# Two more blocks of a gated-linear-attention head turned by transposing transfers instead of by TensorE

## The chip, the cores and the metric

The kernel runs on one core of one Trainium2 chip. The metric is device time in microseconds (us) for one execution, the median of several runs; less is better. TensorE (PE) multiplies matrices into PSUM, VectorE (DVE) and ScalarE (ACT) do the elementwise work, GpSimd (POOL) computes a few square roots here, and SyncE (SP) issues most transfers. ACT issues some transfers too. Each engine runs its own list of instructions in a fixed order, so an instruction that has to wait holds up everything behind it on that engine.

## The reference

A decoder trunk of two layers over 16 learned meta tokens and 512 input tokens, width 1024: first a gated linear attention (GLA) layer with 4 heads, then a differential softmax attention layer with 8 heads, then a final RMSNorm. The part that matters here is the end of the GLA layer. For every head, `o` (528 tokens by 512 columns) is normed by row, multiplied with a gate made from `z`, and multiplied with the output weights:

```python
    o = head_rms(o.transpose(0, 2, 1, 3)).reshape(B, L, D_INNER) * gnorm.astype(f32)
    y = jax.nn.silu(z.astype(f32)) * o
    return (y.astype(xn.dtype) @ w_out)
```

All inputs and outputs are fp32.

## The kernel before, in words

**Layout.** Activations are held transposed: features on the 128 partitions, tokens along the free dimension (`hT`, `s.z`, `s.y`). A product needs its fp32 operands split into a high and a low part, both in the fp32r type; `split` (L261 to 273) does this with one ACT copy (the high part, L270) and one DVE subtraction (the low part, L271), and the product is the sum of three matmul passes.

**Blocks.** The tokens of a head are worked in five blocks (`BLK`): block 0 is the 16 meta tokens, blocks 1 to 4 are 128 tokens each; the last four are the large ones. `gla_blocks` (L1215) goes over them in order. `output(b)` (L1222) multiplies scores and values into a PSUM tile (`ps`; L391, L1233), takes the mean square on ACT (L1236), the inverse root on DVE and POOL (L532, L533), and writes the scaled rows `on` to SBUF (ACT, L1238). The rows stand with tokens on the partitions and have to be turned for the output product.

**Two ways to turn a block.** `rows(b, on)` (L1285) does it on TensorE: four transposes of 128x128 into a PSUM tile (L1291), a DVE product with the gate `s.z` straight from PSUM (L1293), and a split. `far_rows` (L1242) does it for a pair of blocks by transfer: for each block, `leave` copies `on` on ACT so that the two 16-bit halves of each word are apart (L1252, out<-in `t<-t`) and sends them to DRAM from the ACT queue (L1253, `yd<-t`); then `turn` issues one transposing transfer on the SP queue for the pair (L1259, `keep<-yd`), which lands in a part of the buffer `keep` (`b_all`); then `scaled_rows`, once for each block, multiplies in place with the gate on DVE (L1266) and splits. Before the change, blocks 1 to 4 of the second head (`hd == 1`) go by transfer and everything else by `rows`.

**What sets the order.** The program is written out by a generator, the weaver `W`. Attention steps are written where they stand in the code; between them `W.fill(us)` takes pieces of weight products from a queue worth that many estimated microseconds. `W.follow` puts a step behind a stretch of such work: `turn` comes 4.0 us of woven work after the second block has left, and `scaled_rows` a written number of microseconds after that. PE runs exactly in written order. The order on DVE and ACT is set by a scheduler from the written order and priorities; steps marked `urgent` go earlier. `far_rows` is not marked, its `leave` is.

**What runs beside it.** The weight products are `Unit`s (L419 to 511), a seven-product scheme on quarter blocks. Each Unit has partial sums in PSUM tiles `bx`, `by`, `bv`. PE adds p7 to `bx`; ACT copies this partial sum out (`u`, L443); DVE combines it with `bv` (L468); and only after that may PE go on adding p3 into the same `bv` (L422). This is a chain PE, ACT, DVE, PE, and other work of PE (the first product of the next Unit and p4) stands between. Weights come as `raw` tiles (two buffers; SP, L292 and L279), are summed (`sum`, L357) and split to `wh`/`wl` and `a11`, `a12`, `a22`. During the first head's blocks the queue holds the second head's query and key Units; then `q_gla_v(1)` follows, two Units for the second head's values (`t`), then the first head's output product (`q_gla_out(0)`, L959), with the second head's `gla_scores` (L1158: `kd` at L1162 and L1163, score products at L1170 and L1178) and the small `second_layer_setup` (L1076, L1077, L1082) woven in.

Of the kernel before, what the change touches and what calls it, by code (L numbers as in the profile page):

```python
# [209 lines left out]
def trunk(ctx, tc, x, meta, g_norm, gla_w_in, gla_w_gate_up, gla_b_gate, gla_gnorm, gla_w_out,  # L210
# [21 lines left out]
    def T(p, shape, dt, tag, **kw):  # L232
        uid[0] += 1
        return p.tile(shape, dt, tag=tag, name=f"{tag}_{uid[0]}", **kw)
# [68 lines left out]
    W = Weaver()  # L303
# [252 lines left out]
    def tmp():  # L556
        return T(tp, [P, L], F32, "t")


    def words(t):  # L560

        return t.bitcast(U16)
# [203 lines left out]
    for k0 in range(0, KT, 2):  # L766
        if k0 + 2 < KT:
            scaled_pair(k0 + 2)
        i, ks = k0 // 4, slice(k0 % 4, k0 % 4 + 2)
# [210 lines left out]
    for k in range(KT):  # L980
        for n in range(2):
            for i, x in enumerate((X["b11"], b12) if k < 4 else (X["b21"], X["b22"])):
                if k == 0:
                    warm_up((3, 3, 1, 4)[2 * n + i], idle)
                if (k, 2 * n + i) in turns_of:
                    b, half = turns_of[k, 2 * n + i]
# [228 lines left out]
    def gla_blocks(hd, s, fill, last, far):  # L1215
# [25 lines left out]
        def far_rows(pair):  # L1241

            yd = T(dp, [2, P, 2, 512], U16, "yd", bufs=2)
            src = yd.rearrange("m p h c -> (m p h) c")
            i = pair[0] - 1
            raw = b_all[:, i:i + 2, :].rearrange("p m c -> p (m c)")[:, :8 * P].rearrange("p (m c) -> p m c", m=4)
            left = [0, 1]

            @urgent
            def leave(j, on):  # L1250
                pl = words(tmp()[:, :512]).rearrange("p (h c) -> p h c", h=2)
                act.activation(pl, words(on).rearrange("p (c h) -> p h c", h=2), AF.Copy)  # L1252
                act.dma_start(yd[j], pl)  # L1253
                left.remove(j)
                if not left:
                    W.follow((4.0, turn), tag=s)

            def turn():
                tc.keep_in_program_order(sp.dma_start(words(raw), src, transpose=True))  # L1259
                W.follow((10.5 if i == 0 else 16.5, lambda: scaled_rows(0)), (1.5, lambda: scaled_rows(1)), tag=s)  # L1260

            def scaled_rows(j):
                t0, n = BLK[pair[j]]
                y = raw[:, :, j * P:(j + 1) * P]
                with tc.issue_after(W.mark.ins):
                    dve.tensor_tensor(y, y, s.z[:, :, t0:t0 + n], op=ALU.mult)  # L1266
                    for m0, m1, hi, lo in s.groups:
                        split(hi[:, :, t0:t0 + n], lo[:, :, t0:t0 + n], y[:, m0:m1, :])

            return leave  # L1270
# [27 lines left out]
        prev, leave = None, None  # L1298
        for b in range(5):
            W.fill(0.6 if b == 0 else 1.9 if b == 1 else fill[0])  # L1300
            if prev is not None and (b == 1 or not far):
                rows(b - 1, prev)
            prev = output(b)
            if far and b:
                if b % 2:
                    leave = far_rows((b, b + 1))
                leave(1 - b % 2, prev)
            W.fill(fill[1] if b else 1.6)
        if not far:
            W.fill(2.0)  # L1310
            rows(4, prev)

# [17 lines left out]
    for hd in range(G_HEADS):  # L1330
        s = heads[hd]
        last = hd == G_HEADS - 1
# [28 lines left out]
        else:  # L1361
            W.stop = q_gla_v(hd + 1, heads[hd + 1])
        W.land()
        far = hd == 1
        gla_blocks(hd, s, (1.2, 1.2) if last else (0.6, 1.2) if far else (1.9, 1.6), last, far)
        W.finish()
        W.stop = None

# [441 lines left out]
    s = heads[0]  # L1810
# [14 lines left out]
    for hd in range(D_HEADS):  # L1825
        last = hd == D_HEADS - 1
        s = heads[hd]
# [114 lines left out]
```

## Time and profile before

| | |
|---|---|
| median of three runs | 982.9 us (982.31 to 983.34) |
| profiled execution | 981.49 us, of which its span 979.7 us |
| granted TensorE clock, mean | 0.998 |
| PE busy | 965.9 us (99%) |
| DVE busy | 777.5 us (79%) |
| ACT busy | 621.3 us (63%) |
| four transposes of one large block on PE (L1291) | 0.60 us from first start to last end |
| DVE product with the gate (L1293 from PSUM, L1266 from SBUF) | 0.68 us each |
| ACT copy into halves (L1252) | 1.06 us |

The span is the time from the first to the last instruction. Times in a timeline are counted from the span's start; a row gives start, duration, engine, line, operation, out<-in, shapes and a count, and in square brackets how long the engine was idle before it and who ended that. Rows of matmuls overlap: the next group starts before the modelled end of the last, so that the cost of a group on PE is read from start to start. DVE and ACT rows overlap a little too, and are read in the same way. The first head's blocks are worked from about 106 to 138 us, the second head's from about 210 to 236 us.

### The profile page before, as it was taken

The numbers are of one execution on the slowest core, as the hardware profiler recorded it, in microseconds if no ns is written. First come the engines' busy times: TensorE is split into PE (matmuls) and PEld (weight loads), VectorE is DVE, ScalarE is ACT, GpSimd is POOL, SyncE is SP. The second block draws the span as 40 slices with busy tenths as digits, with TensorE's granted clock in tenths as the row PEclk, the third lists the DMA queues.
The fourth block names the chain that finished last, engine by engine and source line by source line (L and its number), as shares of the span: only waits on it lengthen the run. The fifth ranks groups of instructions, "written<-read, shape, count | busy, mean of one in ns | idle before, by whom it ended". The sixth has DMA issues, their size and how long they took to land. (4 is left out here: it accounts for less than half of the span.)

```text
span 979.7 us, 18153 instructions
## 1 busy us (share of the span) xinstructions
PE 965.9 (99%) x7049; PEld 913.1 (93%) x7049; DVE 777.5 (79%) x1584; ACT 621.3 (63%) x1310; POOL 50.3 (5%) x68
## 2 busy tenths in 40 slices
PE   9999999999999999999999999999999999999997
PEld 8999999999999999998999998898998999988896
DVE  7889885887888797566997985977958879677785
ACT  7775755577647656546757774575764667655573
POOL 1000000000000100000001001001010000000001
PEclk9999999999999999999999999999999999999999
DMA  7322224625363122212323425135252351622212
GB/s 195 87 85 61 77 71 130 153 91 129 121 153 120 52 87 87 82 49 87 98 87 106 129 78 156 48 97 140 80 147 86 98 136 53 181 65 77 87 65 86
DMA packets 113226, 98.37 MB, mean 100 GB/s; under 512 B 37341, under 2 KB 99069, under 8 KB 113136
## 3 DMA queue, kind: packets, MB, share of 16 engines
q1 hardware_dynamic: 109680, 90.66, 31.9%
q10 hardware_dynamic: 3456, 6.51, 1.9%
q8 instruction: 57, 0.93, 0.4%
q14 instruction: 33, 0.27, 0.1%
HBM read 83.64 MB, written 8.62 MB: 94 GB/s over the span
## 5 line engine op out<-in xcount | busy, mean ns | idle before, releaser
L271 DVE TENSOR_TENSOR wl<-raw,wh 128x1024 fp32r<-128x1024 f32 x98 | 119.6, 1222 | 24.7 <-ACT wh L270 16.3
L270 ACT ACTIVATE wh<-raw 128x1024 fp32r<-128x1024 f32 x98 | 103.1, 1054 | 52.1 <-PE by L959 23.7
L422 PE MATMUL bv<-x,wh 128*128 128x264 f32 (+1 forms) x656 | 97.8, 287 | 0.8 <-DVE z L470 0.6
L422 PE MATMUL bx<-x,wh 128*128 128x264 f32 (+1 forms) x640 | 95.3, 287 | 0.6 <-ACT u L443 0.4
L422 PEld LDWEIGHTS bv<-x,wh 128*128 128x128 f32 x656 | 86.4, 189 | 1.5 <-DVE z L470 0.9
L422 PEld LDWEIGHTS bx<-x,wh 128*128 128x128 f32 x640 | 84.5, 189 | 2.3 <-ACT u L443 1.2
L443 ACT ACTIVATE u<-bx 128x264 f32<-128x264 f32 (+1 forms) x120 | 45.4, 379 | 28.6 <-PE bx L422 24.9
L271 DVE TENSOR_TENSOR wl<-sum,wh 128x1024 fp32r<-128x1024 f32 x41 | 50.1, 1222 | 15.7 <-ACT wh L270 13.9
L412 PE MATMUL bx<-x,wh 128*128 128x512 f32 (+1 forms) x256 | 62.5, 386 | 0.0
L1712 POOL TENSOR_TENSOR st<-st,mhalf 128x1 f32<-128x1 f32 x32 | 31.5, 985 | 466.4 <-ACT on L1710 444.0
L422 PE MATMUL bv<-x,wl 128*128 128x264 f32 (+1 forms) x328 | 55.2, 285 | 0.1
L422 PE MATMUL bx<-x,wl 128*128 128x264 f32 (+1 forms) x320 | 54.0, 285 | 0.0
L1676 ACT ACTIVATE p<-p,st 128x528 f32<-128x528 f32 (+3 forms) x64 | 36.4, 569 | 25.3 <-DVE st L1674 24.8
L412 PEld LDWEIGHTS bx<-x,wh 128*128 128x128 f32 x256 | 44.5, 188 | 7.9
L270 ACT ACTIVATE wh<-sum 128x1024 fp32r<-128x1024 f32 x41 | 43.2, 1055 | 10.1 <-PE bv L422 4.0
L270 ACT ACTIVATE a11h<-raw 128x512 fp32r<-128x512 f32 x41 | 25.8, 628 | 35.0 <-DMA raw<-in_diff_w_in_dram 15.4
L422 PE MATMUL by<-x,a12h 128*128 128x264 f32 (+1 forms) x320 | 46.5, 285 | 0.0
L422 PE MATMUL bx<-x,a11h 128*128 128x264 f32 (+1 forms) x320 | 46.3, 285 | 0.0
L422 PEld LDWEIGHTS bv<-x,wl 128*128 128x128 f32 x328 | 45.9, 188 | 0.4 <-issue 0.3
L422 PEld LDWEIGHTS bx<-x,wl 128*128 128x128 f32 x320 | 45.2, 189 | 0.7 <-DVE wl L271 0.5
L422 PEld LDWEIGHTS bx<-x,a11h 128*128 128x128 f32 x320 | 42.2, 188 | 0.7
L422 PEld LDWEIGHTS by<-x,a12h 128*128 128x128 f32 x320 | 41.7, 188 | 0.0
(483 smaller groups left out, 2641.2 us busy)
## 6 DMA issues: line engine op xcount, KB each, us to landing
raw<-in_gla_w_in_dram SPq DMA_DIRECT2D x48, 512.0 KB, 4.6
raw<-in_diff_w_in_dram SPq DMA_DIRECT2D x42, 512.0 KB, 4.1
raw<-in_diff_w_in_dram SPq DMA_DIRECT2D x11, 1024.0 KB, 5.7
raw<-in_gla_w_out_dram SPq DMA_DIRECT2D x8, 1024.0 KB, 5.0
raw<-in_diff_w_out_dram SPq DMA_DIRECT2D x8, 1024.0 KB, 6.4
vd<-planes ACTq DMA_DIRECT2D x12, 268.0 KB, 2.7
vd<-keep ACTq DMA_DIRECT2D x8, 264.0 KB, 2.6
T<-bdr SPq DMA_DIRECT2D x8, 264.0 KB, 3.1
```

The lines of the kernel that those rows point to most:

```text
L270: act.activation(hi, src, AF.Copy)
L271: dve.tensor_tensor(lo, src, hi.bitcast(F32), op=ALU.subtract)
L412: pe.matmul(bank, a[:, k, :], b[k] if n0 is None else b[k][:, n0 + i * nn:n0 + (i + 1) * nn], start=n == 0 and ks[0] == 0, stop=n == len(t ...
L422: pe.matmul(bank[:, :x[q].shape[2]], w[p][:, k * P:(k + 1) * P], x[q][:, k, :], start=first and i == 0, stop=i == len(PASSES) - 1, skip_gr ...
L443: W.moved = act.activation(t, self.bx[:, :self.n], AF.Copy, scale=self.sc)
L1676: act.activation(p[:, :nk], p[:, :nk], AF.Exp, scale=-1.0, bias=st[:, m:m + 1], accum_out=st[:, 2 + m:3 + m])
L1712: pool.tensor_tensor(ms, ms, mhalf[:, :1], op=ALU.pow)
```

## The change

For the first head, blocks 1 and 2 are turned by `far_rows` too; blocks 3 and 4, and block 0, stay with `rows`. `far` is now the number of blocks that go by transfer: 2 for the first head, 4 for the second, 0 for the others. The amounts of woven work around the blocks of the first head stay the same. `scaled_rows` of the first head is written 8.0 us of woven work after `turn` where the second head has 10.5.

```diff
             def turn():
                 tc.keep_in_program_order(sp.dma_start(words(raw), src, transpose=True))
-                W.follow((10.5 if i == 0 else 16.5, lambda: scaled_rows(0)), (1.5, lambda: scaled_rows(1)), tag=s)
+                W.follow(((10.5 if hd else 8.0) if i == 0 else 16.5, lambda: scaled_rows(0)), (1.5, lambda: scaled_rows(1)), tag=s)
...
         for b in range(5):
             W.fill(0.6 if b == 0 else 1.9 if b == 1 else fill[0])
-            if prev is not None and (b == 1 or not far):
+            if prev is not None and not 1 < b < far + 2:
                 rows(b - 1, prev)
             prev = output(b)
-            if far and b:
+            if 0 < b <= far:
                 if b % 2:
                     leave = far_rows((b, b + 1))
                 leave(1 - b % 2, prev)
             W.fill(fill[1] if b else 1.6)
-        if not far:
+        if far < 4:
             W.fill(2.0)
             rows(4, prev)
...
-        far = hd == 1
-        gla_blocks(hd, s, (1.2, 1.2) if last else (0.6, 1.2) if far else (1.9, 1.6), last, far)
+        far = (2, 4, 0, 0)[hd]
+        gla_blocks(hd, s, (1.2, 1.2) if last else (0.6, 1.2) if far == 4 else (1.9, 1.6), last, far)
```

On PE, at the output of the first head's block 2 (`ps_4363` before, `ps_4358` after; `t_4303` is block 1's rows, `a11l` a weight of the key Unit, `a22h` one of the query Unit), before:

```order
L422 MATMUL bx_4341<-x_1_77,a11l_4245 128x264 x4
L1291 MATMUL ps_4354<-ident,t_4303 128x128 x4
L391 MATMUL ps_4363<-v_63_472,a_759_3961 128x512
L391 MATMUL ps_4363<-v_64_473,a_759_3961 128x512
L391 MATMUL ps_4363<-v_63_472,a_760_3962 128x512
L391 MATMUL ps_4363<-v_63_472,c_775_4057 128x512
L391 MATMUL ps_4363<-v_64_473,c_775_4057 128x512
L391 MATMUL ps_4363<-v_63_472,c_776_4058 128x512
L1233 MATMUL ps_4363<-vm_62_471,cm_4056 128x512
```

and after:

```order
L422 MATMUL bx_4345<-x_1_77,a11l_4245 128x264 x4
L391 MATMUL ps_4358<-v_63_472,a_759_3961 128x512
L391 MATMUL ps_4358<-v_64_473,a_759_3961 128x512
L391 MATMUL ps_4358<-v_63_472,a_760_3962 128x512
L391 MATMUL ps_4358<-v_63_472,c_775_4057 128x512
L391 MATMUL ps_4358<-v_64_473,c_775_4057 128x512
L391 MATMUL ps_4358<-v_63_472,c_776_4058 128x512
L1233 MATMUL ps_4358<-vm_62_471,cm_4056 128x512
```

The four transposes are gone and nothing takes their place; the same holds in front of block 3's output, and the rest of PE's order is unchanged.

On DVE, some 15 us later, where the value Units of the second head run (`t` is their output, `kd` is made by `gla_scores(1)`, the two L1077 rows belong to the second layer's setup), before:

```order
L271 TENSOR_TENSOR wl_4608<-raw_4220,wh_4607 128x1024
L470 TENSOR_TENSOR t_4663<-by_4645,u_4565 128x264
L271 TENSOR_TENSOR a12l_4684<-raw_4417,a12h_4683 128x512
L271 TENSOR_TENSOR wl_4680<-sum_4619,wh_4679 128x1024
L1162 TENSOR_SCALAR kd_4761<-ks_4485,eL_1012 128x16
L1163 TENSOR_TENSOR kd_4761<-ks_4485,eL_1012 128x384
...
L1077 TENSOR_SCALAR t_4690<-ps_4691 8x328
L1077 TENSOR_SCALAR t_4695<-ps_4696 8x328
L468 SCALAR_TENSOR_TENSOR t_4664<-bv_4666,u_4719 128x264
```

and after:

```order
L271 TENSOR_TENSOR wl_4598<-raw_4220,wh_4597 128x1024
L470 TENSOR_TENSOR t_4659<-by_4638,u_4555 128x264
L1266 TENSOR_TENSOR keep_83<-keep_83,z_1126 128x4x128 x2
L271 TENSOR_TENSOR wl_4676<-sum_4609,wh_4675 128x1024
L1162 TENSOR_SCALAR kd_4757<-ks_4475,eL_1012 128x16
L1163 TENSOR_TENSOR kd_4757<-ks_4475,eL_1012 128x384
...
L271 TENSOR_TENSOR y_818_4288<-keep_83,y_817_4287 128x4x128 x2
L271 TENSOR_TENSOR a12l_4680<-raw_4415,a12h_4679 128x512
L1077 TENSOR_SCALAR t_4686<-ps_4687 8x328
L1077 TENSOR_SCALAR t_4691<-ps_4692 8x328
L468 SCALAR_TENSOR_TENSOR t_4660<-bv_4662,u_4715 128x264
```

(The left-out rows are a second pair of L1162 and L1163, the same in both.) Two gate products and two subtractions now stand ahead of the L468 that reads `bv`, and `a12l` has moved behind them but stays ahead of that L468; the four DVE instructions that did this work for blocks 1 and 2 stood some 20 to 25 us earlier and are gone there.

On SP, around the same stretch, before:

```order
L292 DMA raw_4220<-in_gla_w_in_dram 128x4x256 x2
L292 DMA raw_4417<-in_gla_w_in_dram 128x4x256 x2
L279 DMA raw_4658<-in_gla_w_out_dram 128x4x512
L1166 ISA
L1166 DMA kd_4761<-steep_1_149_1024 128x800
```

and after:

```order
L292 DMA raw_4220<-in_gla_w_in_dram 128x4x256 x2
L292 DMA raw_4415<-in_gla_w_in_dram 128x4x256 x2
L1259 DMA_TRANSPOSE keep_83<-yd_4309 128x4x512
L279 DMA raw_4654<-in_gla_w_out_dram 128x4x512
L1166 ISA
```

The transposing transfer stands between the last input-weight load of the value Units and the first load of output weights. On ACT, two copies into halves (L1252) and two transfers (L1253) are added right behind the L1238 of blocks 1 and 2, and the two copies that split these blocks (L270, `y`) move back, to just before the L443 that feeds the L468 above.

## The prediction

> **What bounds the kernel now.** I read the page's totals first, then the busy time by stretches around the change, then the waits of PE, then single rows of the timeline. The page first:
>
> ```profile
> span 979.7 us, 18153 instructions
> PE 965.9 (99%) x7049; PEld 913.1 (93%) x7049; DVE 777.5 (79%) x1584; ACT 621.3 (63%) x1310; POOL 50.3 (5%) x68
> ```
>
> PE works for all but 14 us of its span, so the end comes nearer only by PE work that goes away, and moves off by each wait that PE gets. The stretches from the first head's block 1 on (columns: PE, PEld, DVE, ACT, POOL, clock, DMA share, GB/s):
>
> ```profile
> 115.00:125.00 10.00, 10.00 (x71) 9.38 (x71) 9.34 (x16) 6.19 (x12) 0.93 (x1) 1.00 0.01 2
> 125.00:135.00 10.00, 10.00 (x70) 9.36 (x69) 7.32 (x14) 5.82 (x12) 0.69 (x2) 1.00 0.34 106
> 135.00:145.00 10.00, 10.00 (x78) 8.93 (x77) 8.71 (x15) 6.17 (x11) 0.40 (x1) 1.00 0.03 3
> 145.00:155.00 10.00, 10.00 (x85) 10.00 (x85) 6.76 (x18) 5.17 (x10) 0.00 (x0) 1.00 0.36 135
> ```
>
> PE has no gap here, at full clock. But DVE is the second engine, 9.34 of 10 us where work is taken off it and 8.71 where work is put on it. Does PE ever wait for DVE in these Units? The row of PE's waits by line, and the instance itself, at 94 us:
>
> ```profile
> PE bv L422 <- DVE z L470: 0.6, 1, 0.6
> ...
> 93.75 0.42 DVE L470 TENSOR_TENSOR z<-bv,u 128x264 f32<-128x264 f32 x1
> 94.22 0.99 PE L422 MATMUL bv<-x,wh 128*128 128x264 f32 x6 [0.64 <-DVE z L470]
> ```
>
> Yes: PE may not add to `bv` while DVE still has to read it, and starts 0.05 us after the read ends (93.75 + 0.42 = 94.17, against 94.22). So a late DVE read of `bv` is a PE stall, and that is what I follow below.
>
> **Step 1, removed from PE: twice four transposes.** Blocks 1 and 2 of the first head, and for comparison block 2's output of the second head, which has no transposes ahead:
>
> ```profile
> 116.65 0.60 PE L1291 MATMUL ps<-ident,t 128*128 128x128 f32 x4
> 117.00 0.94 PE L391 MATMUL ps<-v,a 128*128 128x512 f32 x3
> 117.78 0.86 PE L391 MATMUL ps<-v,c 128*128 128x512 f32 x3
> 122.74 0.60 PE L1291 MATMUL ps<-ident,t 128*128 128x128 f32 x4
> 123.87 1.54 PE L391 MATMUL ps<-v,c 128*128 128x512 f32 x6
> 219.69 0.86 PE L391 MATMUL ps<-v,a 128*128 128x512 f32 x3
> 220.38 0.86 PE L391 MATMUL ps<-v,c 128*128 128x512 f32 x3
> ```
>
> From the first transpose to the `c` products it takes 117.78 - 116.65 = 1.13 us (123.87 - 122.74 = 1.13 again); without transposes 220.38 - 219.69 = 0.69. So each block saves 0.44 by this comparison, or 0.35 (117.00 - 116.65) if only the transposes' own starts count. I take 0.43: the same three products follow in both. Two blocks: **-0.87 us**, lower bound -0.70. [...]
>
> **Step 2, moved on DVE: the stall.** Per block, DVE loses a gate product from PSUM and a subtraction at 117 to 127 us and gets a gate product from SBUF and a subtraction about 143 us. The sum on DVE is nil; the place is not. The rows there now:
>
> ```profile
> 143.32 0.43 DVE L470 TENSOR_TENSOR t<-by,u 128x264 f32<-128x264 f32 x1
> 143.66 0.68 DVE L271 TENSOR_TENSOR a12l<-raw,a12h 128x512 fp32r<-128x512 f32 x1
> 144.26 1.22 DVE L271 TENSOR_TENSOR wl<-sum,wh 128x1024 fp32r<-128x1024 f32 x1
> 145.40 0.23 DVE L1162 TENSOR_SCALAR kd<-ks,eL 128x16 f32<-128x16 f32 x1
> 146.60 0.89 DVE L1077 TENSOR_SCALAR t<-ps 8x328 f32<-8x328 f32 x2
> 147.42 0.41 DVE L468 SCALAR_TENSOR_TENSOR t<-bv,u 128x264 f32<-128x264 f32 x1
> 148.87 0.89 PE L422 MATMUL bv<-x,wh 128*128 128x264 f32 x6
> ...
> 158.37 0.65 PE L422 MATMUL by<-x,a12l 128*128 128x264 f32 x4
> ```
>
> No row has idle time before it: DVE runs from L470 to L468 without a break. L468 is the read of `bv` that PE's p3 needs (148.87). It ends at 147.83; the margin is 148.87 - 147.83 - 0.05 = 0.99 us. Now two L1266 and two subtractions stand ahead of it. Their pace is in the second head:
>
> ```profile
> 244.94 0.68 DVE L1266 TENSOR_TENSOR keep<-keep,z 128x512 f32<-128x512 f32 x1
> 245.54 0.15 DVE L1173 TENSOR_TENSOR t<-ps,short 32x16 f32<-32x16 f32 x1
> ...
> 246.82 0.67 DVE L271 TENSOR_TENSOR y<-keep,y 128x512 fp32r<-128x512 f32 x1
> 247.43 0.67 DVE L1179 TENSOR_TENSOR t<-ps,tri 128x512 f32<-128x512 f32 x1
> ```
>
> 0.60 and 0.61 us from start to start, 2.42 us for four. `a12l` goes behind them but stays ahead of L468, which adds nothing. So L468 is 2.42 us later against PE, 0.99 is covered, and PE waits 2.42 - 0.99 = **+1.43 us** at p3. Both engines come to this place 0.87 us sooner, so the stall doesn't shrink by step 1. Bounds: 0, if DVE finds 1.43 us of gaps earlier (it has them at 125 to 135: 7.32 of 10, but the weights split in between wait for PE and ACT, so I doubt that they move up); above, 2.42 if the margin is used up too. After the stall the rest is shifted as a whole: `a12l`, split by about 148.4 then, is needed at 158.37, and nothing else in this stretch that PE waits for is behind the four.
>
> **Step 3, the transfers.** They cost PE nothing unless L1266 has to wait for the landing. The rows for the durations:
>
> ```profile
> 121.07 0.69 ACT L1238 ACTIVATE t<-ps,st 128x512 f32<-128x512 f32 x1 [0.40 <-POOL st L533]
> 220.44 1.06 ACT L1252 ACTIVATE t<-t 128x1024 uint16<-128x1024 uint16 x1
> 231.14 11.12 SPq L1259 DMA_TRANSPOSE keep<-yd x2
> raw<-in_gla_w_in_dram SPq DMA_DIRECT2D x48, 512.0 KB, 4.6
> yd<-t ACTq DMA_DIRECT2D x4, 256.0 KB, 5.2
> keep<-vd SPq DMA_TRANSPOSE x4, 5.9
> ...
> 109.31 16.13 SPq L292 DMA_DIRECT2D raw<-in_gla_w_in_dram  x4
> 143.47 0.37 SPq L279 DMA_DIRECT2D raw<-in_gla_w_out_dram  x1
> ```
>
> Block 2's rows are ready at 121.07 + 0.69 - 0.43 = 121.3, the copy ends at 122.4, the transfer to DRAM lands 5.2 later at 127.6. SP has by then issued its last input weights (109.31 + 16.13 = 125.4) and the transposing transfer can go; one of the same shape from `vd` lands after 5.9: 133.5. DVE comes to L1266 at 143.32 + 0.34 - 0.87 = 142.8. Nine us in hand. Upper bound: the second head's first transposing transfer is issued at 231.14 and used at 244.94, so it took 13.8 at most, which gives 141.4, still before. SP's next transfer, L279, stands at 143.47 because its buffer is free only then, so what is queued behind the new transfer loses nothing. I put step 3 at 0.
>
> **Step 4, ACT.** Two copies of 1.06 us and two issues are added at 115 to 122, where ACT works 6.19 of 10. Behind the first stands the copy of `u`:
>
> ```profile
> 115.38 0.39 ACT L443 ACTIVATE u<-bx 128x264 f32<-128x264 f32 x1
> 120.18 1.14 PE L422 MATMUL bv<-x,wh 128*128 128x264 f32 x8
> ```
>
> It slips to 116.44, DVE's L468 to about 116.9 to 117.3, and PE adds to that `bv` at 120.18 - 0.43 = 119.75: 2.4 us in hand. Cost 0; from where the delay exceeds 3.5 us it would be one for one. The `y` copies that move back on ACT can start as each L1266 ends, over 2 us before DVE gets to their subtractions.
>
> **Sum.** -0.87 + 1.43 = +0.56 us. The profiled execution of 981.49 us (its span 979.7, 1.8 outside it) would be 982.05; it lies 1.4 under the median of 982.9. Against the median: **983.5 us**. I take 0.2%, 1.97 us, for what a measurement can tell from no change; this is well inside it.
>
> **The rivals.**
>
> - *No stall.* DVE comes to this stretch 1.43 us sooner, since it has lost four instructions before, or L468 still finds its margin. Then only step 1 is left: 982.9 - 0.87 = 982.0. For it speaks DVE's relief at 117 to 127; against it, that the rows of 143 to 147 follow without a break from work that itself waits for PE. 12 in 100.
> - *The landing is late* (the other side). DVE stands at L1266 from 142.8; with a landing after that, L468 and so PE's p3 slip one for one. To be slower by over 1.97 us it needs 1.4 more, so a landing after 144.2, or 16.6 us after the issue at 127.6. The 13.8 bound speaks against it; for it, that the transposing transfer shares its queue with two weight loads of 512 KB just issued. If it took half as long again as that bound, 20.7 us, it would land at 148.3, 5.5 late: 989.0. [...] 6 in 100.
> - *A second stall.* PE catches DVE again further on, at the subtractions for the second value Unit or at `kd`. One more of the same size: 983.5 + 1.4 = 984.9, at the edge. Against it: DVE works 6.76 of 10 from 145 to 155. 6 in 100, half of it beyond 1.97.
> - *Better than step 1*: transposes that also cost PE something at places that I don't see. It would take -1.97, over twice the whole saving. 4 in 100.
>
> **How the numbers follow.** The forecast has the remaining 72 in 100. Within 0.2%: 72 + 12 and part of the second stall, 85. Slower: 11, with the late landing, the worse half of the second stall and something not seen. Faster: 4. The range runs from the case without a stall and the spread of the runs (981.8) to the second stall (985.0).
>
> **What would show it.** These rows change:
>
> ```profile
> L1291 PE MATMUL ps<-ident,t x64: 207/272/279, 111.2 to 419.3; 128*128 128x128 f32 x48, 16*128 16x16 f32 x16
> 147.41 1.14 PE L422 MATMUL by<-x,a22h 128*128 128x264 f32 x8
> ```
>
> PE has 64 - 8 = 56 transposes of L1291, and the products of 147.41 start 0.87 us earlier, at 146.54. PE's waits have a new row, `bv` L422 for DVE `t` L468, of 1 to 1.5 us at about 149. L1266 of the first head starts at 142.8 with no idle time before it; idle time that a transfer ends there would mean the late landing. Without the new PE wait step 2 is wrong; with a PE wait before 140, step 4.

## The result, and the profile after

The changed kernel takes 985.6 us (median; 983.63 to 986.65) where the kernel before takes 982.8 in runs on the same chip: a ratio of **1.0028, 95% interval 1.0018 to 1.0037**. It is 2.85 us slower where 0.56 was forecast, and it lies above the range. A second set of runs gave 1.0029 (1.0019 to 1.0038).

The profiled execution took 985.63 us, 4.14 more than that of the kernel before. Some 1.3 of these 4.14 are chance: the profiled execution of the kernel before lies that much below its median. The page's totals after:

```profile
span 983.8 us, 18147 instructions
PE 966.5 (98%) x7041; PEld 913.0 (93%) x7041; DVE 777.4 (79%) x1584; ACT 624.3 (63%) x1312; POOL 50.0 (5%) x68
```

PE executes 8 matmuls fewer (7041 for 7049), and yet its busy time is longer. So some of PE's work ran slower, and some waits are new. The waits of PE by line (total, times, longest):

```profile
PE bv L422 <- DVE t L468: 1.6, 1, 1.6
PE ps L391 <- DVE aT L271: 1.2, 2, 0.7
...
PE by L422 <- DVE tick L603: 0.5, 1, 0.5
```

The first is the wait of step 2, at the place that the prediction names. The second had one instance of 0.7 us before and now has two. The third is new, and no step of the prediction leads to it. To see what each cost, PE's timeline is laid beside that of the kernel before. The kernel before first, then the changed one:

```profile
148.39 0.65 PE L422 MATMUL by<-x,a22l 128*128 128x264 f32 x4
...
149.97 2.03 PE L1178 MATMUL ps<-qs,ks 128*128 128x128 f32 x16
...
152.57 1.14 PE L422 MATMUL bx<-x,wh 128*128 128x264 f32 x8
...
290.98 1.14 PE L422 MATMUL by<-x,a12h 128*128 128x264 f32 x8
...
902.69 0.28 PE L1705 MATMUL ps<-vm,am 96*128 96x256 f32 x1
```

```profile
147.54 0.65 PE L422 MATMUL by<-x,a22l 128*128 128x264 f32 x4
149.76 0.99 PE L422 MATMUL bv<-x,wh 128*128 128x264 f32 x6 [1.57 <-DVE t L468]
...
150.95 3.37 PE L1178 MATMUL ps<-qs,ks 128*128 128x128 f32 x16
...
155.16 1.14 PE L422 MATMUL bx<-x,wh 128*128 128x264 f32 x8
...
294.32 1.25 PE L422 MATMUL by<-x,a12h 128*128 128x264 f32 x8 [0.50 <-DVE tick L603]
...
906.83 0.28 PE L1705 MATMUL ps<-vm,am 96*128 96x256 f32 x1
```

Up to 148 us the change gains what step 1 says: `a22l` starts at 147.54 against 148.39, 0.85 us sooner. The products of `bv`, which started at 148.87 before, start at 149.76: from 0.85 ahead to 0.89 behind, so the wait moved PE by 1.74. Then a row that nobody forecast: the same 16 score products of L1178 last 3.37 us where they lasted 2.03. The products of `bx` behind them started at 152.57 and start at 155.16 now, 2.59 behind: 1.70 more were lost without any wait. Later, PE loses 0.65 at 294 and 0.85 at 906, each read from the rows next to the wait; between them the distance of the two kernels drifts by about 0.1. The sum: -0.85 + 1.74 + 1.70 + 0.65 + 0.85 = +4.09, the 4.1 by which the two spans differ.

Busy time by stretches says what happened at 151 us (length, PE, PEld, DVE, ACT, POOL, then the granted clock, DMA share, GB/s):

```profile
149.50:151.00 1.50, 1.24 (x11) 1.24 (x11) 1.21 (x4) 0.86 (x1) 0.00 (x0) 1.00 0.07 14
151.00:151.50 0.50, 0.50 (x5) 0.50 (x6) 0.31 (x2) 0.32 (x2) 0.00 (x0) 0.89 0.00 0
151.50:154.50 3.00, 3.00 (x16) 3.00 (x15) 0.31 (x3) 0.00 (x0) 0.00 (x0) 0.50 0.23 90
154.50:155.00 0.50, 0.50 (x5) 0.50 (x4) 0.50 (x1) 0.21 (x1) 0.00 (x0) 0.69 0.00 0
155.00:158.00 3.00, 3.00 (x27) 3.00 (x26) 1.87 (x4) 2.85 (x6) 0.00 (x0) 1.00 0.09 24
```

TensorE's granted clock is still 1.00 when PE works again. Then it is cut to half: 0.89 in a slice of 0.5 us is 0.11 us at half, 0.69 is 0.31, if both are read as a mix of full and half. So it starts at 151.39, 1.63 us after the wait has ended, and lasts 0.11 + 3.0 + 0.31 = 3.42 us. PE is busy all that time (3.00 of 3.00 us from 151.50), at a granted clock of 0.50.

Two questions are left for experiments. Did the wait bring the half clock? And what have the waits at 294 and 906 us, hundreds of microseconds behind the change, to do with it?

### The profile page after: what moved, and what is told of

It is laid out like the page before. It is cut to its first block, busy times and chain, and to the rows that moved or that the text cites. A ratio compares the mean times of both kernels' runs of the same rounds, so it can differ in the third digit from the quotient of the medians.

```text
span 983.8 us, 18147 instructions
## 1 busy us (share of the span) xinstructions
PE 966.5 (98%) x7041; PEld 913.0 (93%) x7041; DVE 777.4 (79%) x1584; ACT 624.3 (63%) x1312; POOL 50.0 (5%) x68
## 5 line engine op out<-in xcount | busy, mean ns | idle before, releaser
L270 ACT ACTIVATE wh<-raw 128x1024 fp32r<-128x1024 f32 x98 | 103.1, 1054 | 54.0 <-PE by L959 23.7
L443 ACT ACTIVATE u<-bx 128x264 f32<-128x264 f32 (+1 forms) x120 | 45.5, 380 | 26.0 <-PE bx L422 22.5
L270 ACT ACTIVATE wh<-sum 128x1024 fp32r<-128x1024 f32 x41 | 43.3, 1055 | 9.4 <-PE bv L422 3.4
L270 ACT ACTIVATE a11h<-raw 128x512 fp32r<-128x512 f32 x41 | 25.8, 629 | 35.4 <-DMA raw<-in_diff_w_in_dram 16.3
```

Of the source, the lines that this page charges most:

```text
L270: act.activation(hi, src, AF.Copy)
L443: W.moved = act.activation(t, self.bx[:, :self.n], AF.Copy, scale=self.sc)
```

## Experiments

Two theories on the first question: T, that the DVE instructions ahead of L468 make PE wait, and that the wait itself brings the half clock; R, that the transfers cost by themselves and the half clock was a chance. In all of them the ratio is to runs of the kernel before on the same chip.

### The changed kernel once more

> The changed kernel a second time, unaltered. Theory T (DVE's moved instructions stall PE, and the stall itself is followed by some 3.4 us of TensorE clock at half): PE waits 1.5 to 1.8 us for DVE at `bv` L422 near 149 us, the clock is near 0.5 for about 3.4 us starting 1 to 2 us after the wait, and L1178 behind it takes 3.4 us against 2.0; time 2.5 to 3 us above the kernel before. Rival R (the half clock in the first profile was a chance of that one execution, and the transfers through DRAM carry the rest): the wait is there, the clock stays at 1.00 from 140 to 160, and yet the time is 2.5 to 3 us above.

Measured: 984.5 us against 981.9, 1.0029 (1.0019 to 1.0038). The rows that answer (PE's timeline, then stretches):

```profile
150.40 1.00 PE L422 MATMUL bv<-x,wh 128*128 128x264 f32 x6 [1.45 <-DVE t L468]
```

```profile
149.00:151.50 2.50, 1.10 (x10) 1.10 (x10) 2.35 (x7) 0.91 (x2) 0.00 (x0) 1.00 0.04 8
151.50:155.00 3.50, 3.50 (x20) 3.50 (x20) 0.48 (x3) 0.46 (x2) 0.00 (x0) 0.56 0.20 77
155.00:158.00 3.00, 3.00 (x25) 3.00 (x24) 2.35 (x3) 2.36 (x4) 0.00 (x0) 0.94 0.02 5
```

The wait and the half clock are there again, in the same order and of the same length. So are the two later waits (0.50 at `by`, 1.06 at `aT`). Not in every execution, it seems: the five of its runs with a mean clock of 0.997 or less have a span of 983.6 us on average, the six others 982.2.

### The four instructions behind the read

```diff
-                W.follow(((10.5 if hd else 8.0) if i == 0 else 16.5, lambda: scaled_rows(0)), (1.5, lambda: scaled_rows(1)), tag=s)
+                W.follow(((10.5 if hd else 13.5) if i == 0 else 16.5, lambda: scaled_rows(0)), (1.5, lambda: scaled_rows(1)), tag=s)
```

> The changed kernel with one number altered: the four DVE instructions of the first head (two gate products, two subtractions) are due 5.5 us of PE work later, so that all four stand behind the read of `bv` in L468. Transfers, ACT copies and removed transposes stay. Theory T: no PE wait at `bv` L422 for L468, no half clock, what is left is the removed transposes: 0.85 us under the kernel before, 981.9 us, ratio about 0.999. Rival R (transfers and copies cost by themselves): still 1.5 us or more above the kernel before, 984.3 or more. A wait that only moves (DVE late for the next read, L468 of `by` or the split of `a22`) would show as a new PE wait within 10 us and 983 to 984.

Measured: 983.5 us against 981.9, 1.0017 (1.0008 to 1.0026). By its distance from the kernel before (1.66 us) this is R's forecast; by its trace it is T's. The PE row at the place, and the one where it loses time next:

```profile
148.01 0.89 PE L422 MATMUL bv<-x,wh 128*128 128x264 f32 x6
...
155.07 1.24 PE L422 MATMUL bx<-x,wh 128*128 128x264 f32 x8 [0.28 <-ACT u L443]
...
903.45 0.73 PE L391 MATMUL ps<-v,aT 128*128 128x256 f32 x4 [1.24 <-DVE aT L271]
```

No wait at `bv`, which starts 0.86 us sooner than in the kernel before; clock 1.00 throughout. Of the 0.86, about 0.4 goes at 155, where ACT's copies to `y` now stand ahead of its copy `u`. So near the change nothing is lost to the transfers. But at 903 PE waits 1.24 us for DVE's split `aT`, as in the changed kernel. All of the 1.7 us that this kernel is slower must come from far away, as 1.5 of the 4.1 us in the changed kernel's profile do. That is the second question, and it is taken up next.

### What stands behind the waits at 294 and 906

Both are the end of a chain: PE waits for DVE, and DVE came late because it waited for a weight load. The DVE rows at 898 us, kernel before:

```profile
898.19 0.69 DVE L357 TENSOR_TENSOR sum<-raw 128x512 f32<-128x512 f32 x1 [3.15 <-DMA raw<-in_diff_w_in_dram]
```

and the kernel with the four instructions behind the read:

```profile
899.56 0.69 DVE L357 TENSOR_TENSOR sum<-raw 128x512 f32<-128x512 f32 x1 [4.66 <-DMA raw<-in_diff_w_in_dram]
```

The load was issued at nearly the same time, 892.42 and 892.27, and landed 1.4 us later. The DMA view of 888 to 900 us (40 slices of 0.3 us: busy tenths, GB/s) suggests why. Before:

```profile
DMA  0000000000000020003777999999999874000000
GB/s 0 0 0 0 0 0 0 0 0 0 0 0 0 0 55 0 0 0 113 113 116 225 369 382 348 318 324 341 358 346 299 290 271 155 28 0 0 0 0 0
```

and with the four behind the read:

```profile
DMA  0000000000000000017789999999999510000000
GB/s 0 0 0 0 0 0 0 0 0 0 0 0 0 0 0 0 0 27 171 133 222 300 410 362 355 358 365 345 379 331 320 200 38 24 24 20 24 28 14 0
```

The DMA view lists a queue of the kind instruction, q8, with one packet in each of these two windows. The page of the kernel before counts it over the whole span (packets, MB, share of the 16 engines' time):

```profile
q8 instruction: 57, 0.93, 0.4%
```

57 packets, 0.93 MB, 0.4% of the 16 engines' time: one of 16 KB about every 17 us, each an estimated 1.1 us of a single DMA engine (0.004 x 16 x 979.7 / 57). I call such a packet a code load; whose instructions it brings, no view says. In the kernel before, one stands alone at 892.2 us (the "2" and "55" ahead of the weight load). In the other it falls at 894.8, inside the weight load (two transfers of 512 KB, issued together). There the bulk of the weights is through at 897.6, but a trickle of 14 to 38 GB/s goes on for two more microseconds; in the kernel before the load runs out at 898.4 without a trickle. A sixteenth of the 350 GB/s ahead of it would be an estimated 22, so this may be one of 16 engines that still had its share to bring; no view shows single engines.

This is theory C, an assumption at this point: **a code load that falls into a weight load makes it land over 1 us later, and where code loads fall hangs on how many instructions PE has had so far.** By it the change, which takes 8 matmuls from PE, shifts the code loads behind 117 us. Rival D is that the added transfers or chance do it. Three pairs of kernels tell them apart; the members of each differ only by four small products that PE executes while it has nothing else to do (each is two matmuls in the profile). First the kernel before with four products less, in two of PE's pauses at 10 to 13 us:

```diff
-    warm_up(3)
+    warm_up(1)
...
-    warm_up(3)
+    warm_up(1)
```

> The kernel before, with four of the dummy products of ones that fill PE's idle time at 10 to 13 us left out (two pauses of 0.7 us instead of 0.3; their results are used nowhere). Nothing else. It has as many PE instructions fewer as the changed kernel (8 records in the profile). Theory C (the place of PE's code loads in time hangs on the count of PE instructions; one that falls into the weight load at 893 to 898 us makes that load land 1.3 us later, and PE waits for the split of it): the code load of 892.2 us comes 2 to 3 us later, inside the weight load, PE waits 1 to 1.3 us at L391 for DVE `aT` near 902, and the time rises by about 1.2 us, ratio 1.0010 to 1.0015. Rival D (the wait at 902 comes from the added transfers or is chance): no change, ratio 0.9995 to 1.0005.

Measured: 983.6 us against 982.0, **1.0016** (1.0007 to 1.0025). Leaving out work that PE did in its pauses makes the kernel 1.55 us slower, a little more than C forecast, with no transfer added. But it is not the forecast wait, and C has only a part of it: in the profiled execution, 1.9 us longer than that of the kernel before, 0.4 were lost at a wait for DVE at 12 us, next to the products left out, and 0.7 at the `tick` wait of 292 us, where the code load had moved from 281.3 to 286.7, behind the issue of the weight load at 282.2; the rest went in small steps from 341 to 677 us; at 902 there was no wait.

Then the run with the four instructions behind the read, with four products more, in PE's wait of 0.9 us at 31 us:

```diff
             wa, wb = ws.use(h)
             banks = pb_pair()
+            if i and pad:
+                warm_up(pad.pop(), banks[0])
```

(The line `pad = [4]` ahead of it is left out here.)

> The run with the four DVE instructions behind the read (late), and four dummy products of ones put into PE's wait of 0.9 us at 31 us (results overwritten), so that PE has as many instructions as in the kernel before. Theory C: the code load near 892 is back where the kernel before has it, ahead of the weight load, the wait of 1.2 us near 902 is gone in most executions, and the time is 1 us under late and 0.3 to 0.8 under the kernel before: ratio 0.9990 to 0.9998. Rival D: as late, ratio 1.0013 to 1.0020.

Measured: 981.7 us against 982.0, **0.9995** (0.9986 to 1.0003), 2.0 us better against the kernel before than without the four products (1.0017). The wait at 902 is gone; one of 0.50 at 291 is new. The two profiled executions, 982.71 and 982.56 us, don't show the gain: the first is the fastest of its kernel, the second among the slowest. The traces tell where the waits are, the medians how much they are worth.

> The changed kernel, its DVE order unaltered, with the four dummy products in PE's wait at 31 us that bring the count of PE instructions back to that of the kernel before. Theory C and T: the wait at `bv` and, in about half of the executions, the half clock remain (-0.85 + 1.7 + 0.8 on average), the later waits at 294 and 906 us mostly go: 1.6 to 2.2 us over the kernel before, ratio 1.0016 to 1.0023, against 1.0029 for the changed kernel. Rival D: as the changed kernel, 1.0027 to 1.0031.

(The same four products in the changed kernel, nothing else.) Measured: 982.2 us against 982.2, **1.0002** (0.9993 to 1.0011), against 1.0029 without them. This went beyond both expectations: with its PE instructions brought back to the number of the kernel before, 7049, the changed kernel is as fast as that. PE's timeline at the change:

```profile
149.24 0.99 PE L422 MATMUL bv<-x,wh 128*128 128x264 f32 x6 [1.27 <-DVE t L468]
...
150.43 2.03 PE L1182 MATMUL ps<-qs,ks 128*128 128x128 f32 x16
```

The wait is there, 1.27 us, and PE is 0.37 behind the kernel before (149.24 - 148.87) where the prediction had 0.56. The score products (now L1182) take 2.03 us: no half clock.

The table has, for all traces of this study, the two weight loads: when SP issued the load, when the code load next to it began (to within 0.12 us), how long after the issue DVE began to read the weights (`landed`; in each case DVE waited for this landing), and what PE then waited for the split weights.

```
                          load at 282 us                   load at 893 us
                          issued  code   landed  PE wait   issued  code   landed  PE wait
before                    281.45  281.3   5.28   -         892.42  892.2   5.77   -
before, four fewer        282.17  286.7   6.63   0.50      894.26  894.1   5.81   -
before, four DVE ops      283.07  287.6   6.90   0.48      894.67  897.3   7.18   1.14
before, six DVE ops       287.07  286.9   6.18   -         898.88  898.7   5.55   -
changed                   284.24  288.8   6.77   0.50      895.78  898.8   6.59   0.52
changed, again            284.89  289.3   6.78   0.50      896.19  899.8   7.10   1.06
changed, pad 4            281.88  281.9   6.94   0.49      894.22  893.9   5.63   -
four behind the read      281.26  281.2   6.08   -         892.27  894.8   7.29   1.24
  and pad 4               281.27  281.7   7.14   0.50      893.96  893.6   5.44   -
  and pad 8               281.25  279.0   5.68   -         894.00  893.8   6.15   -
one ahead, pad 4          281.68  286.1   6.93   0.49      893.35  893.1   5.47   -
one ahead, pad 5          281.65  281.5   5.91   -         892.77  892.6   6.70   0.66
filled 14                 283.90  280.9   5.49   -         896.21  890.9   5.52   -
filled 8                  282.37  280.2   5.37   -         893.31  893.1   6.00   -
```

Where the code load comes at or after the issue, PE waits, 11 times of 11. Where it comes before, PE doesn't wait, 16 times of 17. The landing fits without an exception: it takes 6.59 to 7.29 us in the 12 cases with a wait and 5.28 to 6.18 in the 16 without. In the kernel before, both code loads stand 0.1 to 0.2 us on the right side. What also shows is that the count isn't the whole rule: in the two kernels with DVE instructions added, PE's count was as before and a wait of 1.26 us tipped both loads over, while one of 2.46 tipped neither; and with the four behind the read the code load at 281 us stands where the kernel before has it, with 8 matmuls fewer. What sets the start of a code load is open, and that the padding acts through the code loads alone isn't shown.

### More padding

```diff
-    warm_up(3)
+    warm_up(5)
```

(at both places of the pauses at 11 and 13 us, on top of the four)

> As late_pad4, with four more dummy products of ones in PE's two short waits at 11 and 13 us, so that PE has 8 records more than the kernel before. They may cost up to 0.4 us there. Theory C: code loads come some 2.5 us earlier than in the kernel before; that of 892 lands near 889.5, clear of the weight load that starts at 893, so that no execution has the wait at 902: ratio 0.9988 to 0.9998, unless another code load now meets another weight load that DVE waits for, which would show as a new wait of PE of 0.5 to 1.3 us. Rival D: as late, ratio 1.0015 or more.

Measured: 983.0 us against 982.0, 1.0008 (1.0000 to 1.0017). The load of 893 met no code, as forecast, but barely: the code load came at 893.8, 0.2 us ahead of the issue, and not near 889.5. And at 884 PE now waits 1.07 us for DVE's `v`, and is about 1.2 us later from there on. No kernel with 7041 or 7049 matmuls in its profile waits there; this one has 7057. It is what the last clause of the expectation allows for; that a code load is behind that wait too was not traced.

### One of the four ahead

Against the run with the four behind the read and four products more:

```diff
-                W.follow(((10.5 if hd else 13.5) if i == 0 else 16.5, lambda: scaled_rows(0)), (1.5, lambda: scaled_rows(1)), tag=s)
+                W.follow(((10.5 if hd else 12.5) if i == 0 else 16.5, lambda: scaled_rows(0)), (1.5, lambda: scaled_rows(1)), tag=s)
```

> As late_pad4 (the changed kernel with four dummy products in PE's wait at 31 us), but with one of the first head's two gate products ahead of the read of `bv` in L468 and the other three instructions behind it. In the traces DVE has about 0.6 us in hand there, as much as one of them takes, so no wait or one of 0.2 at most; and ACT's first copy to `y` moves out of the crowd at 148 to 153 us that made PE wait 0.3 us for ACT's `u` at 155 in late and late_pad4. Theory T: PE is 0.7 to 0.85 us ahead of the kernel before from 117 to 280 us; time 0.3 to 0.4 under late_pad4: ratio 0.9987 to 0.9995. Rival: DVE is late by more than 0.3 us and the gain is lost, ratio 0.9995 to 1.0005.

Measured: 982.2 us against 982.2, 0.9999 (0.9990 to 1.0009). The rival was right: there is no wait at `bv`, but the crowd on ACT is worse, not better:

```profile
155.56 1.25 PE L422 MATMUL bx<-x,wh 128*128 128x264 f32 x8 [0.69 <-ACT u L443]
```

All 0.7 us of the saved transposes go at this one wait for ACT's `u`.

> As one_pad4, with a fifth dummy product in PE's short wait at 13 us, which moves the code loads 0.5 us further forward against the weight loads. Theory C: where one_pad4 meets the weight loads of 282 and 893 us in part of its executions (waits of 0.5 and 1.3 us), this one meets them less often: ratio 0.9983 to 0.9993, and less spread. Rival D (the place of the code loads doesn't matter): as one_pad4 within 0.0003.

Measured: 982.5 us against 982.2, 0.9999 (0.9990 to 1.0008). A miss: no gain. (The edit: one of the two `warm_up(3)` is `warm_up(4)`.) Its code load at 281.5 came ahead of the weight load, but at 903 there was a wait of 0.66, the one exception in the table; and after a wait of 0.90 us for DVE at 12 us PE was 0.43 us behind the kernel before when it came to 31 us, where the run before it was level.

### Does the wait bring the half clock?

Work put in the place of the wait, with DVE's order as in the changed kernel:

```diff
-            self.freed = None
+            self.freed, self.idle = None, 0
...
             def p3():
+                if self.idle:
+                    warm_up(self.idle, ps_tile())
                 yield from product(self.bv, ws.use(s43)[0], X["b22"], False)
...
+                if hd == 1 and h == 0:
+                    gens[-1].idle = 14
```

> The changed kernel with 14 products of a 128x128 matrix of ones put on PE right ahead of the waiting products of `bv` (their result is used nowhere); some 0.11 us each, 1.5 us together, so that PE works through what is now its wait. DVE's order ahead of L468 stays. Theory T: PE reaches the same products at the same time, with 0.3 us or less of waiting, the clock stays at 1.00, and L1178 takes 2.0 us again: -0.85 for the transposes, +1.7 for the place of the wait, nothing for the clock: 983.6. Rival R (half clock has nothing to do with PE standing idle, or was a chance): clock and time as in the changed kernel, or 985.5 without any half clock in either.

Measured: 984.5 us against 981.9, 1.0024 (1.0014 to 1.0034); clock 1.00 from 140 to 160, no half clock. But 14 of these products are 28 matmuls, 0.11 us each from start to start, and take 3.1 us, not 1.5, so that PE was later than the wait had made it, and the time says little.

> The changed kernel with 8 instead of 14 dummy products ahead of the waiting products of `bv`: the 14 took 3.1 us from start to start (0.22 each), more than the wait that they were to fill; 8 take 1.75. Theory T: clock 1.00 from 140 to 160, next to no wait at `bv`; against the kernel before -0.85 for the transposes and +1.75 for the filled wait. Theory C: 16 records more bring the code loads back ahead of where the kernel before has them, so no waits at 294 and 906. Together +0.9: 982.8 where the kernel before has 981.9. If the clock has nothing to do with the wait, or if the later waits remain, 984.0 to 984.5.

Measured: 985.0 us against 982.0, 1.0023 (1.0012 to 1.0034), a miss by its time. In the profiled execution (982.46, the fastest of its runs) PE's timeline and the stretch behind it have the forecast:

```profile
149.60 0.98 PE L422 MATMUL bv<-x,wh 128*128 128x264 f32 x6
...
150.78 2.03 PE L1182 MATMUL ps<-qs,ks 128*128 128x128 f32 x16
```

```profile
150.50:154.00 3.50, 3.50 (x33) 3.50 (x32) 1.50 (x5) 1.29 (x3) 0.00 (x0) 1.00 0.22 82
```

PE starts `bv` 0.73 behind the kernel before, without a wait, at full clock. From 150 us on this kernel is 8 matmuls ahead of the kernel before (7057 in all), as the one with pad 8 is, and it has the same wait for DVE's `v` at 884 (0.50 in this execution). What its other executions lose on top was not seen in a trace.

The other way round: the kernel before, with nothing but DVE instructions added ahead of the read.

```diff
+        def extra():
...
+                    for _ in range(2):
+                        dve.tensor_tensor(y, y, s.z[:, :, NM:NM + P], op=ALU.mult)
+            W.follow((12.0, lambda: ops(0)), (1.5, lambda: ops(1)), tag=s)
...
+            elif hd == 0 and b == 2:
+                extra()
```

> The kernel before, with four extra DVE products of the same size (0.6 us each, in place on a buffer that is no longer read; results used nowhere) right ahead of the same read of `bv`; no transfers, no copies, all transposes stay on PE. Theory T: margin 0.99 us, so PE waits 1.4 to 1.6 us at `bv` L422 near 149.9, the clock then goes to half for some 3.4 us, together +3.1 to +3.4: 986.0. Rival R (the loss is the transfers'): the wait, if any, but no half clock; 983 to 984.4.

Measured: 983.7 us against 981.9, 1.0019 (1.0009 to 1.0028). PE's row and the stretches:

```profile
150.23 0.99 PE L422 MATMUL bv<-x,wh 128*128 128x264 f32 x6 [1.26 <-DVE t L468]
```

```profile
149.00:151.00 2.00, 0.77 (x6) 0.77 (x7) 2.00 (x7) 0.67 (x2) 0.00 (x0) 1.00 0.05 11
151.00:154.50 3.50, 3.50 (x32) 3.50 (x32) 1.62 (x6) 1.50 (x3) 0.00 (x0) 1.00 0.23 82
```

The wait comes from the four DVE instructions alone, that part of T holds. The half clock doesn't: a wait of 1.26 us didn't bring it, and the sum of 986.0 was wrong. So the length had to be raised, with three in place of two:

> The kernel before with six instead of four extra DVE products ahead of the read of `bv` (0.6 us each, results used nowhere). Four gave a wait of 1.26 us at `bv` and a clock of 1.00; the two profiles of the changed kernel had waits of 1.57 and 1.45 us and half clock for 3.4 us from 1.7 us after them. Theory T (a wait that is long enough against a fixed stretch of some 3.4 us brings half clock in the next such stretch): the wait is 2.4 to 2.6 us, half clock follows it for about 3.4 us, and the time is 1.2 us for the wait and about 1.7 for the clock over before_dve: ratio to the kernel before 1.0040 to 1.0052. Rival (the half clock in the changed kernel came from something else, such as the transfers' power or chance): 1.2 us over before_dve, clock 1.00, ratio 1.0028 to 1.0035.

Measured: 987.9 us against 982.2, **1.0059** (1.0045 to 1.0073), more than T gave. PE's row and the stretches:

```profile
151.39 1.69 PE L422 MATMUL bv<-x,wh 128*128 128x264 f32 x6 [2.46 <-DVE t L468]
```

```profile
149.00:151.00 2.00, 0.00 (x0) 0.00 (x0) 2.00 (x5) 0.17 (x1) 0.00 (x0) 1.00 0.00 0
151.00:158.00 7.00, 6.61 (x30) 6.61 (x31) 2.34 (x8) 1.35 (x3) 0.00 (x0) 0.52 0.13 44
158.00:160.00 2.00, 2.00 (x18) 2.00 (x17) 1.55 (x3) 1.89 (x3) 0.00 (x0) 0.97 0.00 0
```

Without any transfer added, half clock for 7 us, twice the 3.4: PE was 2.52 us behind the kernel before at the end of the wait and 5.75 at 158 us. So T holds with a length: at this place waits of 1.26 and 1.27 us brought nothing, 1.45 and 1.57 us brought 3.4 us of half clock, 2.46 us brought twice that, and no wait (work in its place) brought none. But the length isn't all. The second trace of the changed kernel has another pause of 1.54 us, early on, and the clock stays at 1.00 behind it:

```profile
12.54 0.44 PE L704 MATMUL bx<-ident,y 128*128 128x128 f32 x2 [1.54 <-DVE y L684]
```

```profile
13.00:16.00 3.00, 2.72 (x25) 2.53 (x24) 2.55 (x7) 2.44 (x7) 0.79 (x2) 1.00 1.15 310
```

The traces show where the two differ, by the times at which the clock changes. In the changed kernel it is at half from 151.39 to 154.81 us and falls again, PE's work being done, at 980.83; in its second trace it falls at 151.94 and 981.38; with the six DVE instructions at 151.30 and 984.15. From fall to fall it is 829.44, 829.44 and 832.85 us: two equal distances, and one that is 3.41 longer, as long as the stretch of half clock. All three are whole multiples (243, 243 and 244) of 3.413 us, and the stretches of half clock are one such step or two. So I read the clock of these traces in steps of 3.413 us. Counted back in these steps (from 980.10 and 978.88, where it falls at the end of the two traces that had no half clock before), the waits of 1.26, 1.27, 1.45 and 1.57 us each lie within one step, and where half clock follows, it begins as that step ends. The pause of 1.54 us is cut by an edge at 11.99 into 0.99 and 0.55. So in these five it looks as if the idle time within one step decides: 1.27 of 3.41 us was too little, 1.45 was enough. Five pauses are few for a rule, and no run moved a pause against the steps while its length stayed.

## Why the prediction was wrong, point by point

What failed is the sum, at two of its terms: the stall of step 2 was priced at its own length, and "After the stall the rest is shifted as a whole" put everything behind it at nothing. What the runs showed in their place stands below, step by step.

**Step 1 was right.** -0.87 forecast, 0.85 measured at 147.54 us. The row of L1291 among the prediction's last lines has a median of 272 ns for one transpose; four of them overlap and take 0.35 us from start to start (116.65 to 117.00), and eight cost no more than 0.85.

**Step 2 named the right wait, and was short by 0.3.** 1.43 us forecast, PE moved by 1.74 in the changed kernel's profile. With the four products of padding it moved by 1.44 (`a22l` started there at 147.32, 1.07 ahead, and `bv` 0.37 behind), which is the forecast. "Both engines come to this place 0.87 us sooner" held there, and not in the changed kernel: its DVE came to L470 at 142.78, only 0.54 sooner. The cause is step 4.

**Step 4, costed at 0, can cost what step 2 lacks.** It looked only at what stands behind ACT's first copy, `u`. Behind the second stands a weight split. Kernel before (ACT, DVE, SP, DVE):

```profile
122.17 1.05 ACT L270 ACTIVATE wh<-raw 128x1024 fp32r<-128x1024 f32 x1
123.26 1.23 DVE L271 TENSOR_TENSOR wl<-raw,wh 128x1024 fp32r<-128x1024 f32 x1
124.52 0.92 SPq L292 DMA_DIRECT2D raw<-in_gla_w_in_dram  x2
131.75 0.68 DVE L357 TENSOR_TENSOR sum<-raw 128x512 f32<-128x512 f32 x1
```

Changed kernel:

```profile
123.19 1.04 ACT L270 ACTIVATE wh<-raw 128x1024 fp32r<-128x1024 f32 x1
124.27 1.23 DVE L271 TENSOR_TENSOR wl<-raw,wh 128x1024 fp32r<-128x1024 f32 x1 [0.16 <-ACT wh L270]
125.52 0.92 SPq L292 DMA_DIRECT2D raw<-in_gla_w_in_dram  x2
131.33 0.69 DVE L357 TENSOR_TENSOR sum<-raw 128x512 f32<-128x512 f32 x1 [0.77 <-DMA raw<-in_gla_w_in_dram]
```

The copy of 1.06 us makes the split 1.0 later, the split frees the `raw` buffer 1.0 later, SP issues the next weight load 1.0 later, and DVE waits 0.77 us for its landing. So DVE is only 0.42 us ahead of the kernel before here, where PE is 0.85 ahead. In the padded kernel DVE waited only 0.47 us for the same load and kept its lead (0.93 us ahead here), so the chain costs between nothing and 0.4 us, by how long the load takes. A delay on an engine that works 6.19 of 10 us came back through a buffer.

**Step 3 was right.** L1266 starts at 143.12 without idle time; the transfer had landed.

**The sum left two things out.** The wait was priced at its own length, but the wait of 1.57 us was followed by half clock, worth another 1.70. And "the rest is shifted as a whole" isn't so: code loads and weight loads move against each other (the code load near 282 us starts 0.1 us ahead of the issue before, 4.6 behind it after), and two loads that DVE has no slack for landed late (6.77 and 6.59 us after the issue, for 5.28 and 5.77 before; 0.65 and 0.85 us of PE in the profile). The padded pair says how much hangs on the second point: four products in a pause, and the changed kernel goes from 1.0029 to 1.0002. Not all of these 2.6 us is the two late waits. In the padded kernel's profile the wait was also 0.3 us shorter, and with that the half clock stayed away; and the wait at 292 was still there. Over all executions, the mean clock tells the two apart as far as it goes. Among those with a mean clock of 0.998 or more, the changed kernel's second set of runs has a span of 982.2 us on average, the kernel before on that chip 980.3; with padding it is 980.4, the kernel before 980.4. So some 1.9 of the 2.6 us are there without a stretch of half clock. How they divide between the late loads and the shorter wait is open.

**The rivals.** "No stall" and "the landing is late" didn't happen. The slower side came from none of the named mechanisms: PE did catch DVE again, as "a second stall" had it, but some 145 and 757 us further on and by way of the transfers. The 85 in 100 for no change rested on a sum whose terms all lie within 50 us of the change; that it should hold for the other 830 us was never argued. The padded changed kernel, at 1.0002, comes nearest to what the sum described, with the wait and no half clock; that its time also agrees is partly luck, since its profile has the late wait of 0.49 us at 292.

No version beats the kernel before by more than the measurement can tell. The best, the four instructions behind the read with padding, is at 0.9995 (0.9986 to 1.0003); against the change as made it is 0.3% faster.

## What to carry to other kernels

Where a kernel's bound engine has no slack, compare the two traces over the whole span before looking for a cause near the edit: an edit that takes instructions away can cost more, far behind it, than it saves (here 0.65 and 0.85 us at 294 and 906, with 0.85 saved at 148). A control kernel with as many instructions as before (a few idle products in an existing pause) helps to tell such a shift from the edit's own effect. And a stall on TensorE isn't priced by its length alone: here from between 1.27 and 1.45 us on, half clock could follow, so look at the granted clock of the microseconds behind it.

## What the runs showed of the hardware

**The clock fell behind some short pauses.** Pauses of PE of 1.45, 1.57 and 2.46 us in the middle of steady work, at about 150 us, were followed by 3.4, 3.4 and 7 us at half clock (0.50 in the slices that lie within). It began 1.54 and 1.63 us after PE had started again, and for the longest pause 0.09 us before; each time a whole number of steps of 3.413 us ahead of the fall at the end of the trace. Behind pauses of 1.26 and 1.27 us at the same place, and behind one of 1.54 us at 12.5 us, cut by the edge of a step into 0.99 and 0.55, the clock stayed at 1.00.

**Weights landed later where a code load fell into their transfer.** 57 code loads of 16 KB in 980 us take only 0.4% of the time of the 16 DMA engines, but with one of them at 894.8 us, inside a pair of 512 KB weight transfers, DVE could read the weights 7.29 us after the issue, where it was 5.77 with the code load just ahead. In the table a small step goes with such a difference: with the code load at 281.5 and the issue at 281.65 the landing took 5.91 us (one ahead, pad 5), with 281.9 and 281.88 it took 6.94 (changed, pad 4). That is 0.17 us between the two, with the start of a code load known to within 0.12; and at the other load of the first of these kernels 6.70 us passed with the code load 0.17 ahead, the one exception. How the one delays the other, no view shows.
